# A two-layer decoder trunk on one core: one raw tile per seven-product pair, slots of three and two blocks, two-bank accumulators, and four k pairs in seven products in five of eleven FFN groups

## The chip, the cores and the metric

The kernel runs on one NeuronCore of a Trainium2 chip. The metric is the device time of one execution, in microseconds (us). The engines are named as in the profile: PE is TensorE (matrix products), PEld its weight loads, DVE is VectorE, ACT is ScalarE, POOL is GpSimd and SP is SyncE, which issues most of the transfers. The profile also gives the clock that PE was granted, as a share of full speed.

## What is computed

A trunk of two pre-norm residual layers over 256 positions of width 2048, in float32. Layer 0 mixes with sliding-window attention and an mLSTM side by side, layer 1 with forgetting attention (FoX); each mixer is followed by a SwiGLU feed-forward network (FFN) with 5632 hidden columns, and a last RMSNorm ends the trunk.

```python
def swiglu(xn, w_gate, w_up, w_down):
    return (jax.nn.silu(xn @ w_gate) * (xn @ w_up)) @ w_down

def reference(x, norm_mix, norm_ffn, norm_final, ...):
    h = x
    for layer in range(DEPTH):                      # DEPTH = 2
        xn = rms_norm(h, norm_mix[layer])
        if layer % 2 == 0:
            mix = swa_mlstm_mixer(xn, ...)
        else:
            mix = forgetting_attention_mixer(xn, ...)
        h = h + mix
        h = h + swiglu(rms_norm(h, norm_ffn[layer]), w_gate[layer], w_up[layer], w_down[layer])
    return rms_norm(h, norm_final)
```

## The kernel before

**Products in two parts.** PE multiplies numbers in a float32 format of reduced precision. So each weight block is loaded in float32 ("raw"), rounded by a cast on ACT to a high part ("hi"), and DVE subtracts the high part from the raw one to give a low part ("lo"). The activations are held in the same two parts: xh and xl for the normalised input (256 positions, 16 blocks of 128 of k), mh and ml for the FFN's hidden values. Each product is three matmuls: high by high, high by low, low by high (`three`, L531). A matmul is 128 x 128 by 128 x 512 and fills one PSUM bank. Every transposition and every weight therefore passes ACT and DVE before PE can use it: a pair of 128-row blocks by 512 columns costs one cast of 1024 elements per partition and one subtraction of 1024 (`split_chunk`, L184).

**Pairs.** `pair_group` (L539) computes two 256 x 512 results at once (two weight matrices, or two column ranges of one), walking over k in pairs of blocks. A pair is plain (kind 0) or of seven products (kind 1). A plain pair multiplies two k blocks by two position halves by two matrices: eight products, 24 matmuls, and two loaded chunks to split. A seven-product pair takes the 2 x 2 by 2 x 2 product in the manner of Strassen and Winograd: seven products, 21 matmuls, with four sums of weight blocks formed on DVE (L607 to L610) and four sums of activation blocks formed beforehand (`sums_of`, kept in sx for the FFN's input and in sd for its hidden values). Three of its products go straight into the four plain accumulators, four into accumulators of their own ("prods"), which `combine` (L553) adds up in a tile c at the end of a group.

**Which pairs are of which kind** is a table: ORDER for the 11 FFN groups (three of eight pairs in seven products, five plain), DOWN for the down projections, MIX tables for the mixers. A second table, HEAVY, with four seven-product pairs, is used for the groups listed in DENSE, which is empty. The sums of activations for the fourth pair (FOURTH = 7) live in unused halves of xh and xl (`rooms`) and in x4.

**The FFN** (`ffn`, L637). Hidden columns come in 11 groups of 512. For each, one `pair_group` computes gate and up; the plain accumulators are added to c (L665), ACT applies Silu (L667), DVE multiplies (L669), and the result is transposed into mh and ml: by DMA for most groups (`join`, run some pairs into the next group), but on PE for the third group (L678 to L690, tile pf), since the down projection comes right behind. After groups 0 to 2, 3 to 6 and 7 to 10 (PARTS) a down projection of two `pair_group` calls adds to the residual h (`add_out`, L758). At the end of layer 0 its `close` also transposes the next layer's input on PE (`split_turned`, `split_scaled`, tile pt).

**Buffers.** A load takes a raw tile of two blocks, 512 KB; in the FFN four raw tiles serve seven-product pairs (RAWS), and a tile t4 holds two of the four sums. Split weights go to eight slots of two blocks, hi and lo (`slot`, `stock`). PSUM has eight banks: four in a pool pa, four in pm. Every accumulator tile is one bank, and a group's plain accumulators and its prods take turns between the pools (`par`), so that the next group can begin in banks that the last one's combine has released.

**Order.** Each engine carries out its own instructions in a fixed sequence, with semaphore waits between engines; DVE, ACT and PE each have one queue. The sequence is set when the program is built, by a scheduler that goes by priorities and estimates, so an edit in one place moves instructions in others. Instructions of SP are the loads, each of which waits for its raw tile's last reader.

Of the kernel before, what the change touches and what calls it, by code (L numbers as in the profile page):

```python
# [7 lines left out]
F32 = mybir.dt.float32  # L8
# [9 lines left out]
P = 128  # L18
D = 2048
S = 256  # L20
# [18 lines left out]
DENSE = ()  # L39
# [15 lines left out]
RAWS = 4  # L55
# [20 lines left out]
def trunk(  # L76
# [27 lines left out]
    stock = []  # L104
# [6 lines left out]

    wr = ctx.enter_context(tc.tile_pool(name="wr", bufs=4))
# [4 lines left out]
    pa = ctx.enter_context(tc.tile_pool(name="pa", bufs=4, space=PSUM))  # L117
    pm = ctx.enter_context(tc.tile_pool(name="pm", bufs=4, space=PSUM))
# [9 lines left out]
    def load_raw(w, k0, c0, n, pool=wr, bufs=4, raws=None):  # L128
        if raws:
            raw = raws.pop(0)  # L130
            raws.append(raw)
        else:
            raw = pool.tile([P, CK, NB], F32, tag="raw", name="raw", bufs=bufs)
        loaded[0] = nc.sync.dma_start(
            raw[:, :, 0:n], w[k0 * P : (k0 + CK) * P, c0 : c0 + n].rearrange("(k p) n -> p k n", p=P)
        )
        return raw
# [28 lines left out]
    ones = cp.tile([P, P], F32, name="ones")  # L166
    nc.gpsimd.memset(ones, 1.0)
    cold = pm.tile([P, NB], F32, tag="pm", name="cold")
    for _ in range(COLD):
        nc.tensor.matmul(cold[:, 0:P], ones, ones, start=True, stop=True)  # L170
    upper = cp.tile([P, P], F32, name="upper")
    nc.gpsimd.affine_select(
        out=upper, in_=ones, pattern=[[1, P]], compare_op=ALU.is_ge, fill=0.0, base=0, channel_multiplier=-1
    )
# [17 lines left out]

    def new_acc():
        return [pa.tile([P, NB], F32, tag="acc", name="acc") for _ in range(NT)]
# [45 lines left out]
    def square_sum(key, n):  # L240
        if n == 0:
            sums[key] = sm.tile([P, NT, 4], F32, tag="ss", name="ss")
        for t in range(NT):
            junk = sm.tile([P, NB], BF16, tag="junk", name="junk", bufs=1)
# [18 lines left out]
    def sums_of(pool, sh, sl, copies, full=None, tags=("tmp", "tmp"), bufs=None, box=None, x4=None):  # L263
# [9 lines left out]
        nc.vector.tensor_tensor(out=s[:, 1, :], in0=s[:, 0, :], in1=full[:, 0, 0, :], op=ALU.subtract)  # L273
        nc.vector.tensor_tensor(out=s[:, 2, :], in0=full[:, 0, 0, :], in1=full[:, 0, 1, :], op=ALU.subtract)
        nc.vector.tensor_tensor(out=s[:, 3, :], in0=full[:, 1, 0, :], in1=s[:, 1, :], op=ALU.subtract)
# [6 lines left out]
    def split_scaled(idx, n, extra=None, joined=None):  # L282
        for half in range(2):
            if joined is None:
                pt = pm.tile([P, 2, NT, P], F32, tag="pm", name="pt")
# [58 lines left out]
    def scrap(fp, n):  # L344
# [5 lines left out]
        else:  # L350
            halves = [fp.tile([P, CK, NB], F32, tag="raw", name="box", bufs=RAWS) for _ in range(2)]
# [3 lines left out]
    def split_plain(dst_h, dst_l, src):  # L355
        nc.scalar.copy(dst_h, src)  # L356
        nc.vector.tensor_tensor(out=dst_l, in0=src, in1=dst_h.bitcast(F32), op=ALU.subtract)  # L357

# [169 lines left out]
    def rooms(m):  # L528
        return m[:, 2:11:4, P:S]
# [6 lines left out]
    def bank(par, name):  # L536
        return pm.tile([P, NB], F32, tag="pm", name=name) if par else pa.tile([P, NB], F32, tag="acc", name=name)

    def pair_group(fp, par, lhs, sums, mats, order, todo=(), halves=None, inner=None, raws=None):  # L539
        plain = [[bank(par, "acc") for _ in range(NT)] for _ in range(2)]  # L540
# [31 lines left out]
        for pos, (kind, pair) in enumerate(order):  # L572
# [21 lines left out]
            if first:  # L594
                prods = [bank(1 - par, "prod") for _ in range(4)]
            ra, rb = (load_raw(w, k0, c0, NB, fp, W_RAWS if halves else RAWS, raws) for w, c0 in mats)
            hg, lg = split_chunk(ra, NB)
            run_due(todo, pos)
            t4 = ra if halves else fp.tile([P, 2, NB], F32, tag="t4", name="t4", bufs=1)
            ta, tb, tc_, td = (  # L600
                (ra[:, 0, :], rb[:, 0, :], rb[:, 1, :], ra[:, 1, :])
                if halves
                else (t4[:, 0, :], t4[:, 1, :], ra[:, 0, :], ra[:, 1, :])
            )
            hu, lu = slot()
            split_plain(hu[:, 1, :], lu[:, 1, :], rb[:, 1, :])
            nc.vector.tensor_tensor(out=ta, in0=rb[:, 0, :], in1=ra[:, 0, :], op=ALU.subtract)  # L607
            nc.vector.tensor_tensor(out=tb, in0=rb[:, 1, :], in1=rb[:, 0, :], op=ALU.subtract)
            nc.vector.tensor_tensor(out=tc_, in0=rb[:, 1, :], in1=ta, op=ALU.subtract)
            nc.vector.tensor_tensor(out=td, in0=ra[:, 1, :], in1=tc_, op=ALU.subtract)  # L610
            parts = []
            for src in (ra, rb) if halves else (t4, ra):
                if halves:
                    hs, ls = halves.pop(0)
                    halves.append((hs, ls))
                else:
                    hs, ls = slot()
                split_plain(hs, ls, src)
                parts.append((hs, ls))
            where = ((0, 0), (1, 0), (1, 1), (0, 1)) if halves else ((0, 0), (0, 1), (1, 0), (1, 1))  # L620
            ht = [parts[a][0][:, b, :] for a, b in where]
            lt = [parts[a][1][:, b, :] for a, b in where]
# [3 lines left out]
            three(prods[0], xa[:, t0], la[:, t0], hg[:, 0, :], lg[:, 0, :], first, last)  # L626
            three(plain[0][0], xb[:, t0], lb[:, t0], hg[:, 1, :], lg[:, 1, :], fresh(0, 0), False)
            three(plain[1][0], sh[3], sl[3], hu[:, 1, :], lu[:, 1, :], fresh(1, 0), False)
            three(prods[1], sh[0], sl[0], ht[0], lt[0], first, last)
            three(prods[2], sh[2], sl[2], ht[1], lt[1], first, last)  # L630
# [746 lines left out]
```

## Time and profile before

| | |
|---|---|
| time, median of 3 runs | 2077.5 us (2077.31 to 2078.14) |
| the profiled execution, whole | 2077.56 us |
| its span, first to last instruction | 2075.9 us |
| granted PE clock, mean | 0.999 |
| FFN of layer 0, about | 370 to 1000 us |
| FFN of layer 1, about | 1385 to 2065 us |

A row of groups reads: line of the kernel, engine, operation, tile written <- tiles read, shape, count | busy time in us, mean ns of one | idle time of the engine just before them and what ended it. A timeline row reads: start, duration, engine, line, operation. A row of waits reads: engine, tile and line that waited <- engine, tile and line waited for: us in all, times, longest. Durations overlap at their ends where an engine is pipelined, so the cost of one more instruction is the distance from start to start, which is shorter than its duration. Where PE is busy all the time, idle time of the others costs nothing.

### The profile page before, as it was taken

The page shows a single profiled execution, that of the slowest core. Times are in us where ns is not written, and L with a number is a line of the kernel's source. Part 1 is how long each engine was busy: PE and PEld are TensorE (multiplying, and loading weights), DVE is VectorE, ACT ScalarE, POOL GpSimd, SP SyncE. Part 2 cuts the span into 40 slices and gives each one's busy share as a digit, 9 for nine tenths or more (in the row PEclk, how much of TensorE's full clock was granted, in tenths as well). Part 3 has the DMA queues.
Part 4 walks back from the last instruction along what each step waited for, and adds up shares of the span by engine and source line. Part 5 has one row for each costly group of instructions (what it writes and reads, how often), then busy time and mean ns, then how long its engine had stood idle before and what let it go on. Part 6 is the DMA issues. An engine that isn't in the chain of part 4 may idle for free.

```text
span 2075.9 us, 26965 instructions
## 1 busy us (share of the span) xinstructions
PE 2065.7 (100%) x9473; PEld 1715.1 (83%) x9473; DVE 1819.0 (88%) x2367; ACT 1373.7 (66%) x1744; POOL 44.6 (2%) x66
## 2 busy tenths in 40 slices
PE   9999999999999999999999999999999999999998
PEld 7878888888888888888888888888888888888886
DVE  6788769999999999999899688689999999999994
ACT  6777678664676656667676776687655666556763
POOL 1010000000000000000000001000000000000000
PEclk9999999999999999999999999999999999999999
DMA  8566577666677666766676776586756677667764
GB/s 292 169 216 192 188 244 238 206 219 196 210 223 224 193 208 217 222 204 183 206 213 209 231 201 183 155 268 217 233 187 218 209 217 224 202 195 225 206 196 141
DMA packets 309576, 434.88 MB, mean 209 GB/s; under 512 B 106412, under 2 KB 114624, under 8 KB 309312
## 3 DMA queue, kind: packets, MB, share of 16 engines
q1 hardware_dynamic: 307088, 426.27, 66.1%
q0 software_dynamic: 1632, 5.80, 0.8%
q8 instruction: 74, 1.21, 0.2%
q10 hardware_dynamic: 720, 1.09, 0.2%
q14 instruction: 62, 0.51, 0.1%
HBM read 408.68 MB, written 2.12 MB: 198 GB/s over the span
## 4 chain that ended last, share of the span: by engine, by line
PE 97%; DVE 1%; ACT 1%; issue 1%; DMA 0%; POOLq 0%; POOL 0%; ACTq 0%; DVEq 0%
PE acc L532 21%; PE acc L534 21%; PE acc L533 21%; PE acc L223 6%; PE acc L222 6%; PE acc L224 6%; PE prod L532 5%; PE prod L533 5%; PE prod L534 5%; PE p L386 1%; PE po L487 1%; ACT s L420 0%; PE po L488 0%; DVE lo L188 0%; DMA raw<-in_w_down_dram 0%
## 5 line engine op out<-in xcount | busy, mean ns | idle before, releaser
L188 DVE TENSOR_TENSOR lo<-raw,hi 128x1024 fp32r<-128x1024 f32 (+3 forms) x656 | 771.1, 1195 | 135.5 <-ACT hi L187 133.0
L187 ACT CAST hi<-raw 128x1024 fp32r<-128x1024 f32 (+3 forms) x656 | 661.7, 1027 | 341.2 <-PE acc L534 137.2
L533 PE MATMUL acc<-lo,xh 128*128 128x512 f32 x1320 | 514.0, 389 | 0.0
L534 PE MATMUL acc<-hi,xl 128*128 128x512 f32 x1320 | 511.4, 389 | 0.0
L532 PE MATMUL acc<-hi,xh 128*128 128x512 f32 x1320 | 506.2, 390 | 0.0
L534 PEld LDWEIGHTS acc<-hi,xl 128*128 128x128 f32 x1320 | 247.8, 188 | 51.6
L533 PEld LDWEIGHTS acc<-lo,xh 128*128 128x128 f32 x1320 | 247.8, 188 | 51.4 <-issue 0.2
L532 PEld LDWEIGHTS acc<-hi,xh 128*128 128x128 f32 x1320 | 247.7, 188 | 51.3 <-issue 0.2
L356 ACT CAST hi<-raw 128x512 fp32r<-128x512 f32 x204 | 166.9, 819 | 160.7 <-PE acc L534 83.6
L357 DVE TENSOR_TENSOR lo<-raw,hi 128x512 fp32r<-128x512 f32 x204 | 191.6, 939 | 11.4 <-ACT hi L356 10.4
L533 PE MATMUL acc<-lo,mh 128*128 128x512 f32 x466 | 181.0, 389 | 0.0
L534 PE MATMUL acc<-hi,ml 128*128 128x512 f32 x466 | 180.3, 389 | 0.0
L532 PE MATMUL acc<-hi,mh 128*128 128x512 f32 x466 | 176.2, 389 | 0.1
L356 ACT CAST hi<-t 128x1024 fp32r<-128x1024 f32 x95 | 100.0, 1053 | 63.9 <-PE acc L534 38.0
L357 DVE TENSOR_TENSOR lo<-t,hi 128x1024 fp32r<-128x1024 f32 x95 | 116.2, 1224 | 15.2 <-ACT hi L356 15.0
L223 PE MATMUL acc<-lo,mh 128*128 128x512 f32 (+1 forms) x322 | 126.3, 392 | 0.0
L222 PE MATMUL acc<-hi,mh 128*128 128x512 f32 (+1 forms) x322 | 125.8, 391 | 0.0
L224 PE MATMUL acc<-hi,ml 128*128 128x512 f32 (+1 forms) x322 | 123.7, 391 | 0.0
L532 PEld LDWEIGHTS acc<-hi,mh 128*128 128x128 f32 x466 | 87.5, 188 | 18.5 <-ACT hi L187 0.5
L534 PEld LDWEIGHTS acc<-hi,ml 128*128 128x128 f32 x466 | 87.5, 188 | 18.2
L533 PEld LDWEIGHTS acc<-lo,mh 128*128 128x128 f32 x466 | 87.4, 188 | 18.2
L223 PE MATMUL acc<-lo,xh 128*128 128x512 f32 (+3 forms) x288 | 100.0, 348 | 0.2 <-DVE lo L188 0.2
(356 smaller groups left out, 3174.7 us busy)
## 6 DMA issues: line engine op xcount, KB each, us to landing
raw<-in_w_gate_dram SPq DMA_DIRECT2D x176, 512.0 KB, 4.5
raw<-in_w_up_dram SPq DMA_DIRECT2D x176, 512.0 KB, 4.6
raw<-in_w_down_dram SPq DMA_DIRECT2D x176, 512.0 KB, 4.8
raw<-in_w_in_odd_dram SPq DMA_DIRECT2D x88, 512.0 KB, 5.3
raw<-in_w_in_even_dram SPq DMA_DIRECT2D x51, 512.0 KB, 5.1
raw<-in_w_out_even_dram SPq DMA_DIRECT2D x32, 512.0 KB, 5.2
raw<-in_w_out_odd_dram SPq DMA_DIRECT2D x32, 512.0 KB, 4.7
hr<-in_w_in_even_dram SPq DMA_DIRECT2D x12, 512.0 KB, 4.5
```

The source lines that it names most:

```text
L187: latest[0] = nc.scalar.copy(hi[:, k, 0:n], raw[:, k, 0:n])
L188: nc.vector.tensor_tensor(out=lo[:, k, 0:n], in0=raw[:, k, 0:n], in1=hi[:, k, 0:n].bitcast(F32), op=ALU.subtract)
L222: nc.tensor.matmul(o, ah[:, ts], hi, start=(k == 0), stop=False)
L223: nc.tensor.matmul(o, ah[:, ts], lo, start=False, stop=False)
L224: nc.tensor.matmul(o, al[:, ts], hi, start=False, stop=(k == k_all - 1 and cs.stop == n))
L356: nc.scalar.copy(dst_h, src)
L357: nc.vector.tensor_tensor(out=dst_l, in0=src, in1=dst_h.bitcast(F32), op=ALU.subtract)
L386: nc.tensor.matmul(pq[j % 2][:, j // 2, :], q_of(j, b), k_of(j)[:, 0:cols], start=True, stop=True)
L487: nc.tensor.matmul(po, v_of(j, 0), tt[:, j, 0:2, :].rearrange("p c q -> p (c q)"), start=True, stop=False)
L532: nc.tensor.matmul(o, ah, hi, start=start, stop=False)
L533: nc.tensor.matmul(o, ah, lo, start=False, stop=False)
L534: nc.tensor.matmul(o, al, hi, start=False, stop=stop)
```

## The change

1. DENSE is now (1, 4, 5, 8, 9): in those five groups of both layers four of eight pairs are of seven products instead of three.
2. In the FFN a seven-product pair loads both matrices into one raw tile of four blocks ("quad", two buffers) in place of two raw tiles and t4. One cast and one subtraction take three blocks at once, into a slot of three blocks ("triple"); the four sums of weights become one double instruction with a repeated operand and two single ones. Eight slots of two blocks become six, beside two triples.
3. Accumulators, prods, pf and pt are tiles of two banks (`two_banks`); pa has two, pm has two in the FFN (`renew_pm`) and four single banks elsewhere. Additions of two banks are one instruction.
4. Block parity in the seven-product form is swapped, so that the spare halves used by `rooms` are others; the tables ones and upper are built anew in each mixer, the scratch tile of the square sums is taken from pools that are there anyway, and an area for descriptors of transfers is halved.

```diff
-DENSE = ()
+DENSE = (1, 4, 5, 8, 9)
...
-RAWS = 4
+QUADS = 2
...
+    def triple():
+        triples.append(triples.pop(0))
+        return triples[-1]
...
-    pa = ctx.enter_context(tc.tile_pool(name="pa", bufs=4, space=PSUM))
-    pm = ctx.enter_context(tc.tile_pool(name="pm", bufs=4, space=PSUM))
+    pa = ctx.enter_context(tc.tile_pool(name="pa", bufs=2, space=PSUM))
+    pms = ctx.enter_context(ExitStack())
+    pm = pms.enter_context(tc.tile_pool(name="pm", bufs=4, space=PSUM))
+
+    def renew_pm(bufs):
+        nonlocal pm
+        pms.close()
+        pm = pms.enter_context(tc.tile_pool(name="pm", bufs=bufs, space=PSUM))
...
+    def two_banks(par, name):
+        return Acc((pm if par else pa).tile([P, NT, NB], F32, tag="pm" if par else "acc", name=name))
...
     def split_scaled(idx, n, extra=None, joined=None):
+        both = two_banks(1, "pt") if joined is None else None
         for half in range(2):
             if joined is None:
-                pt = pm.tile([P, 2, NT, P], F32, tag="pm", name="pt")
+                pt = both[half].rearrange("p (i t q) -> p i t q", i=2, t=NT)
...
     def pair_group(fp, par, lhs, sums, mats, order, todo=(), halves=None, inner=None, raws=None):
-        plain = [[bank(par, "acc") for _ in range(NT)] for _ in range(2)]
+        plain = [two_banks(par, "acc") for _ in range(2)]
...
+                raw = fp.tile([P, 2 * CK, NB], F32, tag="quad", name="raw", bufs=QUADS)
+                for m, (w, c0) in enumerate(mats):
+                    load_raw(w, k0, c0, NB, into=raw[:, CK * m : CK * (m + 1), :])
+                hg, lg = triple()
+                latest[0] = split_plain(hg, lg, raw[:, 0:3, :])
+                hu, lu = hg[:, 2, :], lg[:, 2, :]
+                run_due(todo, pos)
+                nc.vector.tensor_tensor(
+                    out=raw[:, 1:4:2, :], in0=raw[:, 3:4, :].broadcast_to([P, 2, NB]), in1=raw[:, 1:3, :], op=ALU.subtract
+                )
+                nc.vector.tensor_tensor(out=raw[:, 2, :], in0=raw[:, 2, :], in1=raw[:, 1, :], op=ALU.subtract)
+                nc.vector.tensor_tensor(out=raw[:, 0, :], in0=raw[:, 0, :], in1=raw[:, 2, :], op=ALU.subtract)
+                (h1, l1), (h0, l0) = slot(), slot()
+                split_plain(h1, l1, raw[:, 1:4:2, :])
+                split_plain(h0, l0, raw[:, 0:3:2, :])
...
                 for m in range(2):
-                    for t in range(NT):
-                        o = c[:, 2 * t + m, :]
-                        nc.vector.tensor_tensor(out=o, in0=plain[m][t], in1=o, op=ALU.add)
+                    o = c[:, m : m + 3 : 2, :]
+                    nc.vector.tensor_tensor(out=o, in0=plain[m].both, in1=o, op=ALU.add)
...
                 if g == g1 - 1 and nk < 16:
+                    turn_in = two_banks(par, "pf")
                     for half in range(2):
-                        pt = bank(par, "pf").rearrange("p (i q) -> p i q", i=2)
+                        pt = turn_in[half].rearrange("p (i q) -> p i q", i=2)
...
-            more = [[fp.tile([P, CK, NB], F32R, name=f"{a}{i}", bufs=1) for a in ("hi", "lo")] for i in range(2)]
-            stock.extend(more + [slot() for _ in range(6)])
+            triples.extend([fp.tile([P, 3, NB], F32R, name=f"{a}{i}", bufs=1) for a in ("hi", "lo")] for i in range(2))
+            stock.extend([slot() for _ in range(6)])
+            renew_pm(2)
             ffn(layer, fp, sx, x4, sd, key, todo, **rest)
+            renew_pm(4)
...
         def pair_nat(c0, c1, todo=(), order=MIX, inner=None):
             plain, c = pair_group(od, 0, x_of, sums_x, [(wi1, c0), (wi1, c1)], order, todo, halves, inner)
             for m in range(2):
-                for t in range(NT):
-                    o = c[:, 2 * m + t, :]
-                    nc.vector.tensor_tensor(out=o, in0=plain[m][t], in1=o, op=ALU.add)
+                o = c[:, 2 * m : 2 * m + 2, :]
+                nc.vector.tensor_tensor(out=o, in0=plain[m].both, in1=o, op=ALU.add)
```

## What I expected, and why

> **What bounds the kernel now.** I read the profile's page first (engine totals, then the chain that ended last), then the busy time in stretches of 50 us, then PE's waits.
>
> ```profile
> span 2075.9 us, 26965 instructions
> PE 2065.7 (100%) x9473; PEld 1715.1 (83%) x9473; DVE 1819.0 (88%) x2367; ACT 1373.7 (66%) x1744; POOL 44.6 (2%) x66
> PE 97%; DVE 1%; ACT 1%; issue 1%; DMA 0%; POOLq 0%; POOL 0%; ACTq 0%; DVEq 0%
> ```
>
> ```profile
> core 0: us, PE busy (x) PEld busy (x) DVE busy (x) ACT busy (x) POOL busy (x), PEclk, DMA share, GB/s
> 400.00:450.00 50.00, 50.00 (x222) 41.40 (x221) 49.67 (x63) 33.39 (x38) 0.00 (x0) 1.00 0.70 223
> 450.00:500.00 50.00, 49.89 (x224) 41.01 (x223) 46.79 (x56) 27.34 (x31) 0.00 (x0) 1.00 0.63 193
> 950.00:1000.00 50.00, 50.00 (x226) 41.49 (x225) 44.51 (x55) 32.95 (x47) 0.00 (x0) 1.00 0.56 163
> ```
>
> ```profile
> PE cold L170 <- POOL ones L167: 1.2, 1, 1.2
> PE acc L223 <- DVE lo L188: 0.2, 1, 0.2
> PE acc L222 <- ACT hi L785: 0.2, 1, 0.2
> ```
>
> PE is the bound: it is on the closing chain for 97%, and behind its first wait (1.2 us, once) it waits 0.4 us in the whole program. But the margin is thin. In the FFN stretch 400 to 450 DVE is busy 49.67 of 50 us. A kernel whose PE is full and whose DVE is nearly full gains from fewer matmuls only as long as DVE still delivers everywhere in time, so both must be priced.
>
> Prices, by start-to-start distances, since instructions overlap at their ends. PE, 128x512 matmul:
>
> ```profile
> 395.16 0.39 PE L532 MATMUL acc<-hi,xh 128*128 128x512 f32 x1
> ...
> 397.20 1.07 PE L532 MATMUL acc<-hi,xh 128*128 128x512 f32 x4
> ```
>
> Nine steps in 2.04 us: 0.2267 us each; its 0.39 us duration means that a result is complete about 0.16 us after the next one starts. DVE:
>
> ```profile
> 406.13 0.69 DVE L610 TENSOR_TENSOR raw<-raw 128x512 f32<-128x512 f32 x1
> 406.73 0.70 DVE L607 TENSOR_TENSOR t<-raw 128x512 f32<-128x512 f32 x1
> 407.33 0.70 DVE L608 TENSOR_TENSOR t<-raw 128x512 f32<-128x512 f32 x1
> 407.93 1.23 DVE L188 TENSOR_TENSOR lo<-raw,hi 128x1024 fp32r<-128x1024 f32 x1
> 409.07 1.23 DVE L559 TENSOR_TENSOR c<-prod,c 128x1024 f32<-128x1024 f32 x1
> 410.20 1.23 DVE L188 TENSOR_TENSOR lo<-raw,hi 128x1024 fp32r<-128x1024 f32 x1
> 411.33 1.24 DVE L357 TENSOR_TENSOR lo<-raw,hi 128x1024 fp32r<-128x1024 f32 x1
> ```
>
> 512 elements cost 0.602 us, 1024 cost 1.134 us, whether the source is SBUF or PSUM (L559 reads PSUM). The line through both gives 0.336 us for 256, 0.203 for 128 and 1.666 for 1536. The groups bear this out over the whole run:
>
> ```profile
> L188 DVE TENSOR_TENSOR lo<-raw,hi 128x1024 fp32r<-128x1024 f32 x620 | 746.6, 1223 | 124.2 <-ACT hi L187 121.8 <-DMA hv<-room 0.4
> L610 DVE TENSOR_TENSOR raw<-raw 128x512 f32<-128x512 f32 x109 | 75.5, 693 | 0.6
> L665 DVE TENSOR_TENSOR c<-acc,c 128x512 f32<-128x512 f32 x88 | 58.9, 692 | 0.0
> L362 DVE SCALAR_TENSOR_TENSOR xl<-box,gT,xh 128x256 fp32r<-128x256 f32 x36 | 15.9, 483 | 4.0 <-ACT xh L361 4.0
> L187 ACT CAST hi<-raw 128x1024 fp32r<-128x1024 f32 x620 | 639.9, 1050 | 325.1 <-PE acc L534 137.2 <-DMA raw<-in_w_down_dram 30.8 <-PE acc L224 30.7
> L356 ACT CAST hi<-raw 128x512 fp32r<-128x512 f32 x109 | 67.5, 619 | 89.9 <-PE acc L534 80.1 <-DMA raw<-in_w_in_odd_dram 3.3 <-DMA raw<-in_w_up_dram 2.6
> ```
>
> ACT's 1024 cast is 1.05 us, its 512 cast 0.62, so a 1536 cast is put at 1.48.
>
> **The change, part by part.** *Matmuls removed.* In five groups of each of two layers one plain pair (24 matmuls) becomes a seven-product pair (21): 30 fewer, 30 x 0.2267 = **-6.8 us**, all of it on the bound.
>
> *DVE work added.* A plain pair is two subtractions of 1024, 2.27 us. A seven-product pair was three of 1024 and five of 512 (6.41 us); merged it is one of 1536, three of 1024, two of 512 (1.666 + 3.402 + 1.204 = 6.27). So the merging alone saves 0.14 us a pair, and the fourth seven-product pair adds 4.0 us. A dense group has 4 x (6.27 + 2.27) = 34.2 us of splitting, 2.3 for combining the products (L557 to L559), 2.3 for two merged sums, 1.3 for L669 and some 2.5 for turned activations and their sums: 42.6 us of DVE beside 180 x 0.2267 = 40.8 of PE. An undense group has some 38.6 beside 183 x 0.2267 = 41.5. DVE is thus slower than PE in the dense groups and must live from the lead it brings in.
>
> *Handovers.* Accumulators come and go as tiles of two banks, so a matmul that wants one bank waits for the last read of both. Slots for split weights fall from eight of two blocks to six and two of three. Neither costs engine time; they set where DVE's instructions are due. I therefore read the changed kernel's own instruction order and its semaphore waits, and at each place took a PE event, the DVE instructions queued from it up to the one that a later matmul waits for, and PE's work between the two. Where DVE's sum is the larger, PE stands still for the difference, however far ahead DVE was before, because the chain begins with PE; PE's later matmuls queue behind the waiting one, and with them the release of slots for ACT's casts and SP's loads. The order of before, read the same way with the same prices, has just one place where DVE's sum is larger by more than nothing, 0.6 us. In the changed one there are ten:
>
> (A) End of group 2, both layers: its output is transposed on PE (tile pf) ahead of the down projection. Before:
>
> ```profile
> 463.19 0.82 PE L683 MATMUL pf<-ident,c 128*128 128x128 f32 x6
> 463.72 0.59 ACT L356 CAST mh<-pf 128x512 fp32r<-128x512 f32 x1 [0.88 <-PE pf L683]
> 463.76 0.48 PE L534 MATMUL acc<-hi,sd 128*128 128x512 f32 x1
> 464.34 0.69 DVE L357 TENSOR_TENSOR ml<-pf,mh 128x512 fp32r<-128x512 f32 x1 [0.24 <-ACT mh L356]
> 468.48 1.22 DVE L188 TENSOR_TENSOR lo<-raw,hi 128x1024 fp32r<-128x1024 f32 x1
> 468.85 0.39 PE L533 MATMUL acc<-lo,mh 128*128 128x512 f32 x1
> ```
>
> Six transposes take 0.57 us (463.19 to 463.76), the cast starts with their end, ml 0.62 later, and the lo that starts at 468.48 is read by a matmul at 468.85: no slack even now. In the changed order the ten instructions from ml to the awaited lo are, in order, ml 512, raw 1024 (two differences in one), a 1536 split, raw 512, ml 512, raw 1024, raw 512 three times, lo 1024: 0.602 x 6 + 1.134 x 3 + 1.666 = 8.68, with 0.62 ahead 9.30 us. PE has 16 matmuls and four transposes, 3.63 + 0.38 = 4.01. Stall 5.3, twice: **10.6**. The pf tile of two banks adds to it: its second half is transposed only after the first half's ml.
>
> (B) Last pair before the odd layer's output projection: behind the products come four adds of 512, a split of 1024 and a two-bank add of 1024, 0.16 + 2.41 + 2.27 = 4.84; then the projection's first matmul may start, and PE has three matmuls, 0.68: **4.2**, once.
>
> (C) Group 5 to 6, both layers: a cast (1.05) of a slot freed late, then four of 1024, four of 512, one of 1536 (8.61) up to the last read of the products' two banks; 9.82 against 32 matmuls, 7.25: 2.6, twice, **5.1**.
>
> (D) Groups 8 to 10, both layers: 51 DVE instructions between the products of one group and the wait for those of a later one (4 of 1536, 27 of 1024, 16 of 512, 4 of 128: 47.73 + 0.16) against 194 matmuls, 43.98: 3.9, twice, **7.8**. This is the two dense groups' deficit in the flesh.
>
> (E) End of layer 0, where the next layer's input is transposed between down projections: cast 1.48, then one of 1536, two of 1024, two of 512, six of 256 (7.15), 8.79 with 0.16, against 16 matmuls and four transposes, 4.01: **4.8**, once.
>
> (F) Group 1 to 2: 1.05 + 9.14 + 0.16 against 38 matmuls, 8.61, in layer 0; 1.05 + 29.37 + 0.16 against 126, 28.56, in layer 1: 1.7 + 2.0 = **3.8** with rounding.
>
> The chains lie in different stretches of PE's sequence, so they add: 10.6 + 4.2 + 5.1 + 7.8 + 4.8 + 3.8 = 36.3 us.
>
> *Bounds of what the trace doesn't show.* The 1536 form is new. It costs at least a 1024 (1.134) and at most a 1024 and a 512 apart (1.736); I take 1.666, on the line through two sizes. Sixteen stand in the chains: -8.5 with the low end, and 0.4 less for E's cast; +1.1 with the high one. The quads bring one thing more: two buffers instead of four. In A the 1536 split's load may wait for lo of the quad before last.
>
> ```profile
> raw<-in_w_down_dram SPq DMA_DIRECT2D x176, 512.0 KB, 4.8
> ```
>
> 4.8 + 1.48 of cast = 6.3 us, against 4.5 us of DVE work in front of it: late by 0 to 1.8, twice, 3.5 at most; I take 0, since DVE trails by then. SP issues as many instructions as before. The masks built again on POOL (busy 44.6 us), the swapped block parity and the merged ACT casts (ACT has 34% free) I cost at nothing; without that cover ACT's 1.05 us would lengthen C and F only, where it is counted.
>
> **Sum.** 2077.56 (the profiled run; 1.7 us around its span, 0.06 over the median of 2077.5) - 6.8 + 36.3 = **2107 us**; from 2098 (36.3 - 8.9) to 2112 (36.3 + 1.1 + 3.5) by its own unknowns.
>
> **Rivals.** *1. Only the handovers to other stages bite.* C, D and F are small differences of long sums: 47.73 against 43.98 is 8%, and an 8% cheaper DVE queue undoes D. Then A, B and E are left: 19.6 - 6.8, so 2090.4. For it: C, F and D are 16.7 us of 36.3 and hang on the 1536 price. Against: even at 1.134, D has 45.8 against 44.0.
>
> *2. The cover holds (the other side).* DVE's queue reaches every awaited instruction in time and the 30 matmuls are simply gone: 2077.56 - 6.8 = 2070.8. Its place is A, its point: the ten instructions from ml to lo must take under 4.01 - 0.62 = 3.4 us, 0.34 each. Every 512 row above says 0.60. It lives only if a matmul waits for something earlier than I read. Half of the ten places undone leaves no change at best: with B, C, D and F gone and A at half its price, 10.1 - 6.8 is still slower.
>
> *3. PE also runs slower behind each stall.* A, B, D and E are six standstills of about 4 us or more. If the eight matmuls after each take double pitch, 8 x 0.2267 = 1.8 each, 10.9 in all: 2118. Before can't show it: its longest wait is 1.2 us and its clock column is 1.00 throughout. The Trainium skill, "TensorE: Matmul & The Clock Gate", section "Why this matters for your kernels", says that gaps of PE over about 3 us drop its clock to half until it has been busy again for a window. By its window of about 3.4 us that would be an estimated 1.7 us for each such gap; no row here shows it. Against: A's and D's stalls come in pieces, most of them under 4 us.
>
> **How the numbers follow.** Forecast 0.70, rival 1 0.12, rival 2 0.10, rival 3 0.08. The forecast's own range is 2097 to 2113; with most of rival 3 and the inside of rival 1 the range becomes 2089 to 2121, leaving out rival 2 and the ends. A change within 0.2% (4.2 us) can't be told from none. Rival 2 is faster by 0.33%: faster 0.07 of its 0.10, same 0.03; all else is slower, 0.90.
>
> **What would show it.** In the changed profile: 8547 matmuls of 128x512 instead of 8577; PE waits on DVE of 4 to 6 us in all at the pf transposes of both layers, one of about 4 at the odd layer's output projection and one of about 5 at layer 0's end; waits of 2 to 4 us for the last read of a two-bank product tile at groups 5 to 6 and 9 to 10; PE's busy time down in FFN stretches. If DVE's 1536 group has a mean near 1.2 us rather than 1.75, C, D and F shrink. If PE's waits sum to under 7 us, the forecast is wrong; if the clock column falls under 1.00 behind the waits, rival 3 is right.

## The result and the profile after

| kernel | median | lowest to highest | runs |
|---|---|---|---|
| before | 2077.4 us | 2077.3 to 2078.1 | 4 |
| changed | 2156.6 us | 2153.7 to 2159.4 | 4 |

The ratio is 1.038, with an interval of 1.0362 to 1.0398: 79 us slower, where 30 had been forecast. The profiled execution took 2155.98 us; everything below compares its span with that of before, 2154.3 with 2075.9, a difference of 78.4.

The page's totals and the chain that ended last, of the changed kernel:

```profile
span 2154.3 us, 26376 instructions
PE 2084.9 (97%) x9443; PEld 1715.0 (80%) x9443; DVE 1839.4 (85%) x2135; ACT 1373.9 (64%) x1659; POOL 41.0 (2%) x69
PE 59%; DVE 19%; issue 8%; DMA 7%; ACT 6%; SPq 1%; POOL 0%; ACTq 0%; POOLq 0%; DVEq 0%
```

PE ran 30 instructions fewer, as it should (9443 against 9473). Its share of the closing chain fell from 97% to 59%, and DVE, issuing, loads and ACT took the rest. Two sums split the loss. PE's idle time is 2154.3 - 2084.9 = 69.4 us against 10.2 before: **59.2 us of standstill**. And PE was busy 2084.9 us where 2065.7 - 6.8 = 2058.9 were due: **26.0 us of slower work**. 59.2 + 26.0 - 6.8 = 78.4.

Part of the slower work shows in the granted clock. Stretches of 50 us, columns as before:

```profile
400.00:450.00 50.00, 47.07 (x202) 37.73 (x203) 47.41 (x51) 33.22 (x35) 0.00 (x0) 1.00 0.64 206
450.00:500.00 50.00, 42.07 (x178) 33.80 (x177) 45.01 (x46) 23.68 (x24) 0.00 (x0) 0.93 0.56 183
550.00:600.00 50.00, 50.00 (x222) 41.42 (x221) 47.44 (x50) 32.64 (x33) 0.00 (x0) 1.00 0.65 206
1000.00:1050.00 50.00, 44.74 (x191) 36.00 (x190) 39.01 (x47) 28.17 (x42) 0.00 (x0) 0.93 0.40 118
1300.00:1350.00 50.00, 45.58 (x211) 37.80 (x210) 36.95 (x50) 30.97 (x44) 1.75 (x2) 0.97 0.54 156
1550.00:1600.00 50.00, 42.81 (x180) 34.40 (x179) 44.93 (x46) 22.65 (x24) 0.00 (x0) 0.90 0.58 190
```

Between 550 and 600 all is as before; the loss sits in single places: the pf transposes of layer 0 (450 to 500) and layer 1 (1550 to 1600), layer 0's end (1000 to 1050), the odd layer's output projection (1300 to 1350). PE's waits, costliest first:

```profile
PE prod L563 <- DVE ml L387: 12.4, 3, 6.2
PE acc L563 <- DVE c L586: 11.2, 8, 2.1
PE prod L563 <- ACT hi L386: 6.0, 3, 3.4
PE acc L563 <- DVE c L587: 5.9, 10, 2.3
PE prod L564 <- DVE lo L387: 5.5, 6, 1.3
PE acc L563 <- ACT hi L386: 4.8, 6, 1.8
PE acc L250 <- DVE c L1273: 4.4, 1, 4.4
PE pf L720 <- DVE ml L387: 1.9, 2, 0.9
```

Place A in layer 0, on the timeline:

```profile
477.15 0.59 ACT L386 CAST mh<-pf 128x512 fp32r<-128x512 f32 x1 [1.15 <-PE pf L720]
477.77 0.69 DVE L387 TENSOR_TENSOR ml<-pf,mh 128x512 fp32r<-128x512 f32 x1
478.38 1.22 DVE L651 TENSOR_TENSOR raw<-raw 128x1024 f32<-128x1024 f32 x1
478.51 0.66 PE L720 MATMUL pf<-ident,c 128*128 128x128 f32 x4 [0.93 <-DVE ml L387]
480.85 1.47 ACT L386 CAST hi<-raw 128x1536 fp32r<-128x1536 f32 x1 [3.11 <-DMA raw<-in_w_down_dram]
482.35 1.76 DVE L387 TENSOR_TENSOR lo<-raw,hi 128x1536 fp32r<-128x1536 f32 x1 [2.76 <-ACT hi L386]
484.03 0.68 DVE L654 TENSOR_TENSOR raw<-raw 128x512 f32<-128x512 f32 x1
484.63 0.68 DVE L387 TENSOR_TENSOR ml<-pf,mh 128x512 fp32r<-128x512 f32 x1
485.37 0.80 PE L563 MATMUL prod<-hi,sd 128*128 128x512 f32 x1 [6.20 <-DVE ml L387]
485.96 0.63 PE L564 MATMUL prod<-lo,sd 128*128 128x512 f32 x1
486.39 0.63 PE L565 MATMUL prod<-hi,sd 128*128 128x512 f32 x1
...
489.38 0.63 PE L563 MATMUL prod<-hi,sd 128*128 128x512 f32 x1
```

Three things are to be read here. The queue of DVE is the forecast one, in the forecast order, and the second half of pf does wait for the first half's ml (0.93). But DVE stands idle inside it: the 1536 split waits 2.76 us for its cast, and ACT stands idle for 3.11 us before that cast, until the load is there. And when PE starts again at 485.37 its steps are 0.43 us (485.96, 486.39) until 489.38: half speed for 4 us.

### The profile page after: what moved, and what is told of

Same layout as the page of the kernel before. It is cut to its first block, busy times and chain, and to the rows that moved or that the text cites. A ratio compares the mean times of both kernels' runs of the same rounds, so it can differ in the third digit from the quotient of the medians.

```text
span 2154.3 us, 26376 instructions
## 1 busy us (share of the span) xinstructions
PE 2084.9 (97%) x9443; PEld 1715.0 (80%) x9443; DVE 1839.4 (85%) x2135; ACT 1373.9 (64%) x1659; POOL 41.0 (2%) x69
## 4 chain that ended last, share of the span: by engine, by line
PE 59%; DVE 19%; issue 8%; DMA 7%; ACT 6%; SPq 1%; POOL 0%; ACTq 0%; POOLq 0%; DVEq 0%
PE acc L563 12%; PE acc L564 11%; PE acc L565 11%; DVE lo L387 6%; PE acc L251 5%; PE acc L250 5%; PE acc L252 5%; DMA raw<-in_w_up_dram 4%; DVE lo L213 4%; PE prod L563 3%; PE prod L564 3%; PE prod L565 3%; ACT hi L386 2%; DVE raw L651 2%; ACT c L741 1%
## 5 line engine op out<-in xcount | busy, mean ns | idle before, releaser
L212 ACT CAST hi<-raw 128x1024 fp32r<-128x1024 f32 (+3 forms) x541 | 543.1, 1022 | 312.8 <-PE acc L565 150.8
L213 DVE TENSOR_TENSOR lo<-raw,hi 128x1024 fp32r<-128x1024 f32 (+3 forms) x541 | 633.4, 1184 | 120.2 <-ACT hi L212 118.8
L386 ACT CAST hi<-raw 128x1024 fp32r<-128x1024 f32 (+2 forms) x329 | 379.0, 1169 | 263.9 <-DVE raw L651 62.1
L387 DVE TENSOR_TENSOR lo<-raw,hi 128x1024 fp32r<-128x1024 f32 (+2 forms) x329 | 446.7, 1365 | 100.7 <-ACT hi L386 100.1
L563 PE MATMUL acc<-hi,xh 128*128 128x512 f32 x1260 | 490.9, 393 | 17.6 <-DVE c L586 11.2
L564 PE MATMUL acc<-lo,xh 128*128 128x512 f32 x1260 | 492.2, 391 | 1.1 <-DVE lo L387 1.1
L565 PE MATMUL acc<-hi,xl 128*128 128x512 f32 x1260 | 490.6, 390 | 0.0
L564 PEld LDWEIGHTS acc<-lo,xh 128*128 128x128 f32 x1260 | 237.1, 188 | 52.2 <-DVE lo L387 2.1
L651 DVE TENSOR_TENSOR raw<-raw 128x1024 f32<-128x1024 f32 x105 | 127.7, 1217 | 0.3
L250 PE MATMUL acc<-hi,xh 128*128 128x512 f32 (+3 forms) x288 | 100.0, 347 | 1.1 <-ACT hi L212 1.1
```

Of the source, the lines that this page charges most:

```text
L212: latest[0] = nc.scalar.copy(hi[:, k, 0:n], raw[:, k, 0:n])
L213: nc.vector.tensor_tensor(out=lo[:, k, 0:n], in0=raw[:, k, 0:n], in1=hi[:, k, 0:n].bitcast(F32), op=ALU.subtract)
L250: nc.tensor.matmul(o, ah[:, ts], hi, start=(k == 0), stop=False)
L386: cast = nc.scalar.copy(dst_h, src)
L563: nc.tensor.matmul(o, ah, hi, start=start, stop=False)
L564: nc.tensor.matmul(o, ah, lo, start=False, stop=False)
```

## Experiments

Letters in the expectations name theories, not the places A to F of the prediction. Theory B: two-bank tiles. Theory Q: the single raw tile with its slots. Rival D: the dense groups. Medians stand against the kernel before as measured beside them (2077.3 to 2078.0). Each edit also lets the scheduler order the engines anew, so a difference between two runs holds the new order too.

**Which of the three parts costs: e1 to e7.**

e1, the kernel before with the dense groups alone:

```diff
-DENSE = ()
+DENSE = (1, 4, 5, 8, 9)
```

> The kernel before with DENSE = (1, 4, 5, 8, 9) and nothing else of the change: 30 matmuls fewer, one-bank accumulators, two raw tiles and eight slots. Theory B (the cost sits in the handovers of two-bank tiles): no new handover, so the 6.8 us are mostly kept, 2071 to 2079 us. Rival D (the dense groups' DVE deficit, 42.6 us of DVE beside 40.8 of PE, sets the time): most of the 79 us shows here too, 2110 to 2150. Rival Q (late loads into two quads): no quads here, 2071 to 2079 as by B.

Measured 2093.0 (ratio 1.0073, 1.0056 to 1.0090): 15 us slower, between the theories. The 6.8 us are there, and some 22 are paid for them.

e2, the changed kernel without them:

```diff
-DENSE = (1, 4, 5, 8, 9)
+DENSE = ()
```

> The changed kernel with DENSE empty again: two-bank tiles, quads and triples, three seven-product pairs in every group. Theory B: the handovers stay, so most of the loss stays; the chains in its instruction order that begin with PE and outlast it sum to 27 us against 37 in the changed kernel, and the changed kernel lost 85 (79 plus the 7 saved) where its chains gave 37, so about 60 us: 2125 to 2145. Rival D: back to 2077 to 2090. Rival Q: 2100 to 2140, the quads being there with one fewer per dense group.

Measured 2145.7 (1.0323, 1.0308 to 1.0339): 68 of the 79 us are there without a dense group. Rival D alone falls; theory B's range ended just below.

e3, the changed kernel with one-bank accumulators:

```diff
-        return Acc((pm if par else pa).tile([P, NT, NB], F32, ...))
+        return [(pm if par else pa).tile([P, NB], F32, ...) for _ in range(NT)]
...
-    pa = ctx.enter_context(tc.tile_pool(name="pa", bufs=2, space=PSUM))
+    pa = ctx.enter_context(tc.tile_pool(name="pa", bufs=4, space=PSUM))
...
-                    nc.vector.tensor_tensor(out=o, in0=plain[m].both, in1=o, op=ALU.add)
+                    for t in range(NT):
+                        o = c[:, 2 * t + m, :]
+                        nc.vector.tensor_tensor(out=o, in0=plain[m][t], in1=o, op=ALU.add)
```

> The changed kernel with every accumulator tile cut back to one bank (four in each PSUM pool) and the merged additions taken apart again; quads, triples and the dense groups stay. Theory B: chains of 9 us instead of 37, so 2078 to 2095. Rival Q: most of the loss stays, 2120 to 2150. Rival D: 2130 to 2160.

Measured 2129.7 (1.0254, 1.0238 to 1.0269): 27 us better than the changed kernel, but 52 remain, far above the 18 that theory B allowed and in rival Q's range.

e4, the changed kernel with two raw tiles, t4 and eight slots:

```diff
-                raw = fp.tile([P, 2 * CK, NB], F32, tag="quad", name="raw", bufs=QUADS)
...
-                hg, lg = triple()
-                latest[0] = split_plain(hg, lg, raw[:, 0:3, :])
...
+                ra, rb = (load_raw(w, k0, c0, NB, fp, RAWS) for w, c0 in mats)
+                hg, lg = split_chunk(ra, NB)
...
+                t4 = fp.tile([P, 2, NB], F32, tag="t4", name="t4", bufs=1)
+                hu, lu = (m[:, 0, :] for m in slot())
+                split_plain(hu, lu, rb[:, 0, :])
...
-            stock.extend([slot() for _ in range(6)])
+            stock.extend(more + [slot() for _ in range(6)])
```

> The changed kernel with the quads and triples taken back (four raw tiles of two blocks, t4, eight slots of two blocks, eight DVE instructions a seven-product pair); two-bank tiles and dense groups stay. Theory B: chains of 32 us, so most of the loss stays, 2125 to 2150. Rival Q: 2078 to 2100. Rival D: 2130 to 2160.

Measured 2142.4 (1.0311, 1.0295 to 1.0326). Only 14 us come back: theory Q alone falls too, and theory B's range holds here.

e5, both structures taken back (the edits of e3 and e4 together, so the merged residual addition is taken apart too, other than the expectation says); the other small edits and the dense groups are kept:

> The changed kernel with both structures taken back, one-bank accumulators and two raw tiles with eight slots; the dense groups and the small edits stay (swapped block parity, rebuilt masks, scratch tile, merged residual addition). If the small edits cost nothing, as predicted: like the kernel before with the dense groups alone, 2088 to 2098 us. Rival: the small edits carry part of the loss, 2100 or more.

Measured 2096.4 (1.0091, 1.0076 to 1.0106), within 4 us of e1's loss (19 against 15), and the two intervals overlap: the small edits are near free.

e6 and e7, each structure alone (e3 and e4 with DENSE empty):

> Quads, triples and six slots with one-bank accumulators and no dense group. Theory Q (the quads' loads come late, whatever the groups): 2078 plus the 37 that they added to the dense kernel, 2105 to 2120. Rival QD (they cost only beside the dense groups' DVE deficit): 2078 to 2090.

> Two-bank accumulators with two raw tiles, eight slots and no dense group. Theory B (handovers): 2078 plus the 49 that they added to the dense kernel, 2110 to 2130; its order has chains of 15 us, at the pf tiles, at the odd layer's output projection and at layer 0's end. Rival BD (two-bank tiles cost only where DVE is behind in dense groups): 2080 to 2095.

Measured 2102.0 (1.0120, 1.0103 to 1.0136), 3 us under theory Q's range, and 2116.0 (1.0183, 1.0168 to 1.0198), in theory B's. Side by side, as the difference from before:

| | no dense group | dense groups |
|---|---|---|
| as before | 0 | +15 (e1) |
| quads, triples, six slots | +24 (e6) | +52 (e3) |
| two-bank tiles | +38 (e7) | +64 (e4) |
| both | +68 (e2) | +79 (changed) |

The rows below the first hold the small edits too. All three parts cost, the two-bank tiles most. Alone they cost 24 + 38 + 15 = 77 us and together 79, but that is no proof that they add: in pairs they cost more than their sums, 52 against 39, 64 against 53 and 68 against 62, and the third part then costs less than it does alone.

**How a two-bank tile costs: e8 and e11.** In e8 the products that are read first share a tile:

```diff
-                    prods = [b for _ in range(2) for b in two_banks(1 - par, "prod")]
+                    one, two = (two_banks(1 - par, "prod") for _ in range(2))
+                    prods = [one[0], two[0], two[1], one[1]]
```

> The changed kernel, with the four product accumulators spread over their two two-bank tiles otherwise: the ones that combine reads first (products 0 and 3) share the tile that the next group asks for first. Nothing else is changed. Theory B: PE's waits for the last additions of combine (17 us in the changed kernel's profile) shrink to a third or less, 2135 to 2149. Rival: those waits only pass the lag on to the next split, 2150 to 2162.

Measured 2182.9 (1.0508, 1.0492 to 1.0523): 26 us worse, outside both ranges. PE's waits for the last two additions of combine, 11.2 and 5.9 us in the changed kernel, are 12.9 in all, not a third, and its waits for casts of weights on L386 rose from 10.8 to 19.7. That the scheduler reordered everything around the edit is as likely a reason as the edit itself, so this run says nothing of the tiles except that a new pairing is no remedy.

e11 takes e7 and gives three pairs of banks a tile each, using one bank of it:

```diff
-                    turn_in = two_banks(par, "pf")
+                    turn_in = [two_banks(par, "pf")[0] for _ in range(2)]
...
-                        acc = new_acc()
+                        acc = [two_banks(n - 2, "acc")[0] for _ in range(2)]
```

> Run e7 (two-bank accumulators alone) with three pairs of banks no longer in one tile: the two halves of pf, and the two accumulators of each of the last two output quarters, each get a tile of their own, of which one bank is used. Theory B2 (a two-bank tile is waited for as a whole, by readers of the finished bank and by writers of the free one): the pf waits (7 us) fall to half or less, the first addition at the very end no longer waits for the other half, the stretch behind the last matmul is 2 to 3 us shorter; 2100 to 2110. Rival: the waits come from DVE's queue alone, 2113 to 2119.

Measured 2109.2 (1.0154, 1.0140 to 1.0168), 7 us better than e7. The waits at pf, of e7 and then of e11:

```profile
PE prod L562 <- DVE ml L386: 7.1, 3, 4.0
```

```profile
PE prod L562 <- DVE ml L386: 0.5, 2, 0.4
PE acc L250 <- DVE c L1270: 5.7, 2, 4.4
```

The wait at pf is down from 7.1 to 0.5, the one at the odd layer's output projection, which was not touched, is still 4.4. The other edit shows behind the last matmul. The first addition to h there, in before, in the changed kernel and in e11:

```profile
2063.45 0.69 DVE L1299 TENSOR_TENSOR h<-acc,h 128x512 f32<-128x512 f32 x1 [12.22 <-PE acc L224]
```

```profile
2143.55 1.35 DVE L1342 TENSOR_TENSOR h<-acc,h 128x512 f32<-128x512 f32 x3 [14.03 <-PE acc L252]
```

```profile
2094.61 0.69 DVE L1339 TENSOR_TENSOR h<-acc,h 128x512 f32<-128x512 f32 x1 [13.85 <-PE acc L252]
```

In before the first half's addition stands alone, some 4 us ahead of the last matmul (which starts at 2067.28); in the changed kernel all three additions come in a row after the last matmul (2143.24), although by the same order of matmuls the first half's bank was complete some 4 us earlier; in e11 it is alone again (last matmul 2098.44). The stretch from the start of the last matmul to the end is 8.6 us, 11.0 us and 8.9 us; in e7, from which e11 was made, it is 11.7. So in these programs a two-bank tile is waited for as a whole, by a reader of its finished bank here, by a writer of its free bank at pf.

The place with the 4.4 us is less simple. The changed kernel at place B, PE and then DVE:

```profile
1324.40 0.39 PE L565 MATMUL acc<-hi,xl 128*128 128x512 f32 x1
1329.20 0.50 PE L250 MATMUL acc<-hi,mh 128*128 128x512 f32 x1 [4.42 <-DVE c L1273]
```

```profile
1326.20 0.68 DVE L597 TENSOR_TENSOR c<-prod,c 128x512 f32<-128x512 f32 x1
1326.80 1.21 DVE L213 TENSOR_TENSOR lo<-raw,hi 128x1024 fp32r<-128x1024 f32 x1
1327.93 2.34 DVE L1273 TENSOR_TENSOR c<-acc,c 128x1024 f32<-128x1024 f32 x2
```

PE starts when the first of the two-bank additions that begin at 1327.93 has ended (1.13 us later, 1329.06). The same place in before, from the last product on:

```profile
1277.97 0.39 PE L534 MATMUL prod<-mh,sx 128*128 128x512 f32 x1
1280.14 0.68 DVE L1230 TENSOR_TENSOR c<-acc,c 128x512 f32<-128x512 f32 x1
1281.37 0.39 PE L222 MATMUL acc<-hi,mh 128*128 128x512 f32 x1
```

There DVE frees the first bank with its third addition, ahead of the last two of the products, and PE has 14 matmuls between the last product and the projection; e3, with one-bank tiles in the otherwise changed kernel, has the same order and no wait. In the changed kernel the addition stands behind all four and a split, and PE has three matmuls. So the 4.4 us come with two-bank tiles, but through the order that the scheduler gave them; how much of it is the merged wait is not shown.

In e7's profile the 38 us are 25.3 us more of PE's idle time (35.5 against 10.2) and 13.8 more of its busy time (2079.5 against 2065.7). e11 takes back 7; the rest is not traced to single tiles.

**How the quads cost: e9, e10, e13, e14.** All without dense groups and with one-bank tiles, as e6. e9 keeps the quads and takes the triples back to eight slots; e10 adds a third quad; e13 keeps triples and six slots and takes the three-block cast and subtraction apart; e14 is e9 with six slots:

```diff
# e9
-                hg, lg = triple()
-                latest[0] = split_plain(hg, lg, raw[:, 0:3, :])
...
+                hg, lg = slot()
+                latest[0] = split_plain(hg, lg, raw[:, 0:2, :])
+                hu, lu = (m[:, 0, :] for m in slot())
+                split_plain(hu, lu, raw[:, 2, :])
...
+            stock.extend(more + [slot() for _ in range(6)])
# e10, beside e9
-QUADS = 2
+QUADS = 3
# e13, beside e6
-                latest[0] = split_plain(hg, lg, raw[:, 0:3, :])
+                latest[0] = split_plain(hg[:, 0:2, :], lg[:, 0:2, :], raw[:, 0:2, :])
+                split_plain(hg[:, 2, :], lg[:, 2, :], raw[:, 2, :])
# e14, beside e9
-            stock.extend(more + [slot() for _ in range(6)])
+            stock.extend([slot() for _ in range(6)])
```

> Run e6 (quads alone, no dense group, one-bank accumulators) with the triples and six slots taken back to eight slots of two blocks; the two quads stay, the cast and subtraction of three blocks come apart again. Theory Q1 (the raw tiles: two quads are freed too late, so loads come late): still 2095 to 2105 us. Theory Q2 (too few slots for split weights): 2076 to 2084.

> Run e9 with a third quad, in the memory that the triples held. Theory Q1: the time that ACT's casts wait for loads of gate and up (129 us in e6) falls to about a third, and the time to 2076 to 2084. Theory Q2: as e9.

> Run e6 (quads, triples and six slots, one-bank accumulators, no dense group) with the cast and the subtraction of three blocks taken apart into two blocks and one, into the same triple. Theory Q3 (the form of three blocks: ACT's cast must wait for the second matrix's load and holds up ACT's and DVE's queue for 1.5 and 1.7 us): 2078 to 2086 us, as with eight slots in e9. Theory Q2 (the number and turn of the slots): 2098 to 2106, as e6.

> Run e9 (quads, no triples) with six slots of two blocks instead of eight. Theory Q2: a seven-product pair takes four of six slots, DVE's lead shrinks by a quarter, 2100 or more. Theory Q3: the count matters little, 2080 to 2090.

Measured: e9 2082.4 (1.0025, 1.0014 to 1.0036), e10 2080.5 (1.0015, 1.0006 to 1.0025), e13 2088.2 (1.0053, 1.0038 to 1.0068), e14 2115.7 (1.0184, 1.0167 to 1.0201). The number of quads (theory Q1) is worth 2 us, and the intervals of e9 and e10 overlap. The form of three blocks is worth 14 (2102.0 to 2088.2, slots and quads the same), so theory Q3 holds in kind, though its range ended 2 us lower. The remaining 6 down to e9 go with the slots: e14 is in theory Q2's range, and taking two of eight slots away without triples costs 33. So both theories hold, each for a part. The 5 us that e9 still lies over before (3 with e10's third quad) are not taken apart. The casts of e6, and then of e13:

```profile
L386 ACT CAST hi<-raw 128x1536 fp32r<-128x1536 f32 x95 | 140.8, 1482 | 184.1 <-DMA raw<-in_w_up_dram 129.4 <-DMA raw<-in_w_down_dram 35.7 <-PE prod L565 18.8
```

```profile
L386 ACT CAST hi<-raw 128x1024 fp32r<-128x1024 f32 x285 | 297.9, 1051 | 248.0 <-PE acc L565 112.5 <-DMA raw<-in_w_gate_dram 52.4 <-PE prod L565 35.6
L386 ACT CAST hi<-raw 128x512 fp32r<-128x512 f32 x109 | 67.5, 619 | 30.9 <-DMA raw<-in_w_up_dram 12.2 <-PE acc L565 10.8 <-DMA raw<-in_w_down_dram 6.4
```

The three-block cast needs a block of the second matrix (up), so ACT waited 129.4 us for that matrix's load; taken apart, the two blocks of the first matrix (gate) go as soon as they are there, and the waits are 52.4 for gate and 12.2 for up. In the changed kernel DVE waits in turn:

```profile
L387 DVE TENSOR_TENSOR lo<-raw,hi 128x1536 fp32r<-128x1536 f32 x105 | 184.2, 1754 | 77.7 <-ACT hi L386 77.1
```

These 77.1 us of waiting, on an engine that is busy for 85% of the span, are what the chains of the prediction did not hold; how much of them reaches PE depends on the place.

**What a dense group costs: e12.** The kernel before, DENSE = (4, 8).

> The kernel before with DENSE = (4, 8), two separate dense groups in each layer: 12 matmuls fewer, 2.7 us. If an undense group behind each gives DVE time to recover (slack of some 2.9 us a group against a deficit of 1.8): 2074 to 2078. If every dense group costs what it did in e1 (15 + 7 us for ten of them, 2.2 each): 2082 to 2086.

Measured 2078.1 (1.0002, 0.9993 to 1.0011): the 2.7 us saved are paid back, no gain and no loss. For four of its ten dense groups e1's 22 us would be 9, and e12 pays some 3, so dense groups do not all cost alike. That e1's stand side by side is not the reason: its longest waits between groups are behind group 1, which has no dense neighbour (2.21 us in layer 0, 2.22 in layer 1), while behind groups 4 and 5 the next group starts 0.67 us late. e12 leaves group 1 out. In layer 0, whose first FFN matmul is at about 320 us and not at 370, the wait behind group 1 is not for DVE:

```profile
399.75 0.62 ACT L356 CAST hi<-raw 128x512 fp32r<-128x512 f32 x1
400.27 1.05 ACT L356 CAST hi<-t 128x1024 fp32r<-128x1024 f32 x1
401.21 0.62 ACT L356 CAST sd<-s 128x512 fp32r<-128x512 f32 x1
401.73 0.58 ACT L555 COPY c<-prod 128x512 f32<-128x512 f32 x1
402.37 0.50 PE L532 MATMUL acc<-hi,xh 128*128 128x512 f32 x1 [2.21 <-ACT c L555]
```

PE waits until ACT has copied the first product out of PSUM, and that copy stands in ACT's queue behind three casts. What makes the queue late there is not shown. No version beat the kernel before.

## Why the prediction was right and wrong

**Right: direction, cause in kind, and the places.** The 30 matmuls saved what they should, and PE stands still at the six places named. PE's recorded waits there, against the forecast:

| place | forecast | measured |
|---|---|---|
| A, pf transposes, both layers | 10.6 | 14.1 |
| B, odd layer's output projection | 4.2 | 4.4 |
| C, group 5 to 6, both layers | 5.1 | 5.6 |
| D, groups 8 to 10, both layers | 7.8 | 9.5 |
| E, end of layer 0 | 4.8 | 5.3 |
| F, group 1 to 2, both layers | 3.8 | 7.7 |
| sum | 36.3 | 46.6 |

(B, for one, is the 4.42 of the row above; A is 0.93 + 6.20 in layer 0 and 0.93 + 6.02 in layer 1.) B, C and E were right to half a microsecond. The price of the 1536 form, 1.666 us by the line through two sizes, fits: at A the next instruction starts 1.68 us later (482.35 to 484.03).

Two readings at A were off. The matmul at 468.85 in before cannot read the lo that starts at 468.48, for that ends only at 469.70, so that pair does not show that before had no slack there. And in the changed kernel PE stops already for the fifth of the ten instructions, the second ml: the product that it starts at 485.37 takes over the banks of pf. The awaited lo, five instructions later, is hidden behind PE's half speed. So the queue at A was the forecast one, but the stall was ended by another instruction of it.

**Wrong: the sum held too little, in four terms.** The sum gave 2107.1 us, and the profiled execution took 2156.0. Of the 48.9 us between them, 26.0 are slower work, 10.3 more standstill at the six places, 12.6 standstill elsewhere. So the chains found the places, and held 29.5 of the 78.4 us in the net.

*The loads of the quads.* "Late by 0 to 1.8, twice, 3.5 at most; I take 0, since DVE trails by then." This step failed in its mechanism. At A the split came 2.76 us late, beyond the bound, because the bound priced one load behind one release, and the cast waits for both loads of its quad: it began 7.2 us after the release (473.6 to 480.85), not 4.8. And it was not two places: DVE waited 77.1 us behind 105 such casts. e13 shows the form's price by itself, 14 us of e6's 24. At F, the place furthest above its forecast, the wait is in pieces: for a cast on L386 (1.10 us in layer 0, 1.45 in layer 1), for a subtraction on L387 (1.28 and 0.80) and for combine (1.27 in each).

*Slower work after a standstill.* This is the largest term, and the sum put it at nothing. It stood as rival 3, with 10.9 us and a chance of 0.08, as if it were an alternative; it is a term of the same sum, and 26.0 us large. By the prediction's own sign, a clock column under 1.00 behind the waits, it is right. Part is half speed: the clock is under 1.00 in just the stretches with the long waits. Over 50 us 0.93, 0.93, 0.97 and 0.90 in the rows above, and 0.97 in each of two more stretches, are some 34 us at half clock, at most 17 us lost, fewer where PE stood still anyway: the steps of the 128x512 matmuls in them are 12.1 us longer in all than at 0.2267 each. The rest is the wait's own edge: the last matmul before it runs out to its 0.39 us, with no next one to overlap it (7.6 us in all), and the first one behind it takes 0.47 to 0.50 us instead of 0.39 (3.7 us in all); some 3 us of the 26.0 are not taken apart. Place B lost 4.57 us between its two rows, not 4.42, and from 1329.20 the next steps were longer again. The Trainium skill, "TensorE: Matmul & The Clock Gate", section "Why this matters for your kernels", warns of gaps over about 3 us; the trace agrees in kind, with a shorter gap (below).

*Waits outside the chains.* 59.2 - 46.6 = 12.6 us of idle time lie elsewhere. 2.4 us of it are the stretch behind the last matmul (11.0 against 8.6 us), where a two-bank tile keeps the first addition back; the tail was not looked at, since the chains ended at PE. The rest is single waits, the longest 2.32 us, for combine's last addition between groups 0 and 1 of layer 0; most are for DVE, some for ACT's queue, which the chains held only as one cast.

*Two-bank tiles as such.* "Neither costs engine time; they set where DVE's instructions are due" was right, and was priced only where DVE's queue outlasts PE. e7 shows 38 us for them without any dense group, in place of some 15 from chains in its order; of the missing 23 us, 13.8 are slower work again.

**The rivals.** Rival 1 and rival 2 are out: all six places bite, and more. The account of the dense groups, "DVE is thus slower than PE in the dense groups", fits the sign of e1 (15 us slower, in the net), but the density is the smallest of the three parts, and in e1 PE waits longer for ACT (9.0 us) than for DVE (5.6), so that DVE's deficit is the cause there is not shown. The range ended at 2121 since it had room for most of rival 3's 10.9 us beside the price of the forms and two late loads, and none for waits outside the chains.

## What to carry to other kernels

An instruction that merges two waits (a cast over two loads, a tile over two banks) starts with the later one and frees with the later one; on a kernel whose first engine is full, such a delay can reach that engine at a handover, and saved instructions on a second engine need not pay for it. A chain of counted instructions from one event of the full engine to its next wait gave a lower bound for the stall at all six places, and at the three short ones, B, C and E, a good one (the stall was 5 to 10% longer). To make a time of it, the loads and the third engine's queue have to go into the chain, and each stall has to be charged with its restart and its slow clock, here 26.0 us on 59.2.

## What the runs showed of the hardware

A gap of 6.20 us on PE was followed by about ten matmuls at 0.43 us a step, as shown above. Shorter gaps did it too. e1, PE:

```profile
1466.57 0.39 PE L532 MATMUL acc<-hi,xh 128*128 128x512 f32 x1
1469.18 0.79 PE L532 MATMUL acc<-hi,xh 128*128 128x512 f32 x1 [2.22 <-ACT c L555]
1469.77 0.63 PE L533 MATMUL acc<-lo,xh 128*128 128x512 f32 x1
...
1472.33 0.43 PE L534 MATMUL acc<-hi,xl 128*128 128x512 f32 x1
```

and in the changed kernel even

```profile
1971.42 0.79 PE L563 MATMUL acc<-hi,xh 128*128 128x512 f32 x1 [1.84 <-ACT hi L386]
```

while a gap of 2.21 us in e1 (the row at 402.37 above) was followed by full speed. What decides can be read from the traces' record of the granted clock. In every run all changes of the clock lie on one grid of 3.413 us (to 0.004 us), and in the changed kernel each of the six stretches at half clock lasts one, two or three steps of it (3.41, 6.83 or 10.24 us). The clock changes at the end of a step, by PE's idle time in that step. The gap before 1469.18 left 2.03 us of idle time in the step that ended at 1468.99, the one before 1971.42 left 1.79 us in the step that ended at 1971.35; the gap before 402.37 lay across the end of a step, with 1.75 us in the next, and the clock stayed. Over all sixteen traces the clock fell 46 times, the end of the program aside, 44 of them behind a step with 1.72 us or more of idle time by the profile's modelled ends (1.46 and 1.56 in the other two), and it stayed full behind no step with more than 1.82 us. So about half a step of idle time is enough, and for gaps of about 2 us it depends on where in the grid they fall. The Trainium skill, "TensorE: Matmul & The Clock Gate", section "What's actually happening", tells of a free-running window of 3413 ns, and the grid agrees.
